# The token forms of the second down group: when their splits are issued in a hybrid encoder block

## The chip, the cores and the metric

The kernel runs on one core of a Trainium2 chip. The metric is the device time of one launch in microseconds (us). The engines of the core are TensorE (PE in the profile, with PEld for its weight loads), VectorE (DVE), ScalarE (ACT), GpSimd (POOL) and SyncE (SP). Each works through its own list of instructions in order and waits for the others by semaphores. DMAs are issued by SP, ACT and POOL.

## The reference

One layer over 512 tokens of width 2048, all in float32: an input projection, two attention mixers, an output projection, and a SwiGLU feed-forward part with a final norm. The change touches only the down projection, the last matrix product:

```python
h2 = rmsnorm(x, g_ffn[layer])
gate, up = jnp.split(jnp.einsum('bsd,df->bsf', h2, w_gate_up[layer]), 2, axis=-1)
x = x + jnp.einsum('bsf,fd->bsd', jax.nn.silu(gate) * up, w_down[layer])
return rmsnorm(x, g_final)
```

Here s is 512, d is 2048 and f is 5632.

## The kernel before

**Precision.** TensorE multiplies in a reduced type. So each float32 operand is split into a high half (a cast on ScalarE) and a low half (operand minus high half, on VectorE), and one product is three matmuls: high by high, high by low, low by high (lines 238 to 240).

**Fewer products.** The large products are computed by a scheme of Strassen's kind: a 2 x 2 block product with seven multiplications, named m1 to m7. Each needs one "form" of the tokens (a sum or difference of token blocks) and one of the weights. The token forms live in SBUF in the tiles `arena`, already split. The weight forms are made just before use: for m1, m2 and m3 a weight tile is taken as it was loaded; for m7, m6, m5 and m4 VectorE first makes a sum or difference of two tiles (line 837), and then the split follows (line 795 on ScalarE, line 798 on VectorE).

**Blocks and units.** A `ColBlock` covers a number of pairs of 128-row blocks of the inner dimension. A unit is one form with one pair: six matmuls of 128 x 512. The down projection's inner dimension is cut into three groups of 6, 8 and 8 pairs (`DOWN_PAIRS`), and each group has two blocks, one for each half of the output columns (cb 0 and 1). A block of 6 pairs has 42 units, one of 8 pairs 56. Within a block the units stand in the order m1, m7, m6, two units of m2, m5, the rest of m2, m4, m3. The weights of a unit are split about five units ahead of its matmuls (`COLS_AHEAD`), through a ring of eight tiles `tw`, so at unit n VectorE and ScalarE work on the weights of unit n + 5.

**PSUM.** Several forms share a bank: m1, m6, m5 and m3 one pair of banks, m7 and m4 a second, m2 a third. After the last unit of most forms, ScalarE copies the bank out (`ev`, line 1180) and GpSimd adds the copy to the result in DRAM by an accumulating DMA (`x1d`, line 1181). The next form on the same bank may start only when the copy is done.

**Token forms of the next group.** The gate/up part stores all token forms in DRAM. The arena holds one group's forms at a time, so while the second column block of a group runs, and the first block of the next, `next_forms` brings in the next group's forms one by one: a DMA into a buffer `fr` (two buffers, issued by ScalarE, line 1154), the high half on ScalarE (line 1157) and the low half on VectorE (line 1160). A form of 8 pairs takes two such steps of 4 pairs (h = 0 and 1). So the second group has 14 steps. They are hung on units: `box.after(form, late, f)` runs f behind the matmuls of the unit that is `late` units after the last unit of that form in the block `box`.

**Weight loads.** SP issues one DMA of 256 KB for each weight tile (`raw`, line 267), some 15 units ahead at most and as far as buffers are free. The loads of SP and the `fr` loads of ScalarE take their completion semaphores (DMAHW0 to DMAHW7) from one set of eight in turn. A DMA waits, on the engine that issues it, until the last DMA on its semaphore has landed.

Of the kernel before, what the change touches and what calls it, by code (L numbers as in the profile page):

```python
# [51 lines left out]
W_TILES = {"wi": 10, "wo": 12}  # L52
DOWN_PAIRS = (6, 8, 8)
ORDER = ("m1", "m7", "m6", "m2", "m4", "m5", "m3")
EARLY = 2
EVICT = 6
HEAD_RATE = (1.42, 1.9)
# [5 lines left out]
def f32(ap):  # L63
    return ap.bitcast(F32)
# [3 lines left out]
def encoder_block(ctx, tc, x, g_mix, w_in, g_q_a, g_k_a, g_out_a, g_out_b, w_out, g_ffn,  # L68
# [77 lines left out]
    gqk = turning[:, :2 * HD].rearrange("p (a c) -> p a c", a=2)  # L146
    arena = [sp.tile([P, n, 8, 2, 256], F32R, tag=f"arena{n}", bufs=1, name=f"arena{n}") for n in (EARLY, 7 - EARLY)]

    def form_tile(m, pairs):
        return arena[0][:, m, pairs] if m < EARLY else arena[1][:, m - EARLY, pairs]  # L150

    def form_pair(m, pairs, j):
        t, lo = (arena[0], m) if m < EARLY else (arena[1], m - EARLY)
        return t[:, lo:lo + 2, pairs, j]
# [93 lines left out]
    def in_turn(tiles, n, shape, dtype, tag):  # L248
        if not tiles and homing[0]:
            whole = sp.tile([P, n] + shape[1:], dtype, tag=tag + "s", bufs=1, name=nm(tag))  # L250
            tiles.extend(whole[:, i] for i in range(n))
        if not tiles:
            tiles.extend(sp.tile(shape, dtype, tag=tag, bufs=n, name=nm(tag)) for _ in range(n))
        tiles.append(tiles.pop(0))
        return tiles[-1]
# [49 lines left out]
    def hook(n, f):  # L305
        hooks.setdefault(n, []).append(f)
# [459 lines left out]
    def form_of(form, i):  # L766
        t = form_tile(ORDER.index(form), i)
        return t[:, 0], t[:, 1]
# [259 lines left out]
    def h_side(i, half, apart=False):  # L1028
# [12 lines left out]
        if half >= 2:  # L1041
            src = hpart[0][:, 256:].rearrange("p (f c) -> p f c", c=256)
            for t, part in ((arena[0], src[:, :EARLY]), (arena[1], src[:, EARLY:])):
                if half == 2:
# [91 lines left out]
    for f in range(0, NFF, 4):  # L1136
        box = gate_up_block(f)
# [6 lines left out]
    def next_forms(box, first, pairs):  # L1144
        seq = sorted(CHAIN, key=box.at.get)

        def ready(form, h):
            m, st = ORDER.index(form), {}
            lo_q, n = 4 * h, min(4, pairs - 4 * h)
            hi, lo = (form_tile(m, slice(lo_q, lo_q + n))[:, :, j] for j in range(2))  # L1150

            def load():
                st["t"] = in_turn(frs, 2, [P, 4, 256], F32, "fr")[:, :n]
                nc.scalar.dma_start(st["t"], forms_dram[:, m, first + lo_q:first + lo_q + n])

            def split_hi():
                nc.scalar.activation(hi, st["t"], AF.Copy)

            def split_lo():
                nc.vector.tensor_tensor(lo, st["t"], f32(hi), op=OP.subtract)  # L1160
            late = 4 * seq.index(form) + 4 * h
            box.after(form, late - 5, load)
            box.after(form, late + 1, split_hi)
            box.after(form, late + 3, split_lo)
        for form in seq:
            for h in range(-(-pairs // 4)):
                ready(form, h)
# [120 lines left out]
    first = 0  # L1288
    for n in DOWN_PAIRS:
        next_forms(box, first, n)  # L1290
        for cb in range(2):
            box = down_block(first, n, cb, (first + n, cb) == (NFF // 2, 1))
        first += n

    at = [0.0]
# [145 lines left out]
```

## Time and profile before

| what | us |
|---|---|
| median of 3 runs | 1996.07 (1995.02 to 1996.52) |
| the profiled execution | 1998.18 |
| its span, from the first to the last instruction | 1996.4 |
| TensorE busy in the span | 1979.4 |
| VectorE busy | 1560.5 |
| ScalarE busy | 1106.1 |

Busy time of TensorE is modelled, since matmuls are pipelined: a matmul of 512 columns is shown with 0.39 us, while the next one may start 0.23 us after it. So lost time is better read from the starts of matmuls than from the busy share. The mean granted clock of TensorE over the span is 0.998 of full speed. In the rows of the timeline the first number is the start in us from the begin of the span, the second the duration, and the bracket at the end tells how long the engine had been idle and what ended that.

### The profile page before, as it was taken

The page shows a single profiled execution, that of the slowest core. Times are in us where ns is not written, and L with a number is a line of the kernel's source. Part 1 is how long each engine was busy: PE and PEld are TensorE (multiplying, and loading weights), DVE is VectorE, ACT ScalarE, POOL GpSimd, SP SyncE. Part 2 cuts the span into 40 slices and gives each one's busy share as a digit, 9 for nine tenths or more (in the row PEclk, how much of TensorE's full clock was granted, in tenths as well). Part 3 has the DMA queues.
Part 4 walks back from the last instruction along what each step waited for, and adds up shares of the span by engine and source line. Part 5 has one row for each costly group of instructions (what it writes and reads, how often), then busy time and mean ns, then how long its engine had stood idle before and what let it go on. Part 6 is the DMA issues. An engine that isn't in the chain of part 4 may idle for free.

```text
span 1996.4 us, 27478 instructions
## 1 busy us (share of the span) xinstructions
PE 1979.4 (99%) x9020; PEld 1631.5 (82%) x9020; DVE 1560.5 (78%) x2787; ACT 1106.1 (55%) x1983; POOL 147.2 (7%) x191
## 2 busy tenths in 40 slices
PE   9999999999999999999999999999999999999998
PEld 7888888888888888888888888888888887788886
DVE  6887876668845698877878878878879987887968
ACT  7655345456543565554555555555556665666655
POOL 0000111101110000000000000000000121111121
PEclk9999999999999999999999999999999999999999
DMA  8576532335253555845836747647558799768864
GB/s 276 179 279 234 178 117 94 111 131 186 96 174 113 199 186 175 282 152 196 300 117 248 251 134 263 220 168 277 170 188 286 195 243 261 200 156 269 196 173 153
DMA packets 229216, 390.62 MB, mean 196 GB/s; under 512 B 21408, under 2 KB 70352, under 8 KB 228944
## 3 DMA queue, kind: packets, MB, share of 16 engines
q1 hardware_dynamic: 204592, 325.61, 48.2%
q0 software_dynamic: 17680, 41.95, 9.2%
q10 hardware_dynamic: 6800, 21.31, 3.1%
q8 instruction: 70, 1.15, 0.2%
q14 instruction: 74, 0.61, 0.1%
HBM read 325.08 MB, written 63.70 MB: 195 GB/s over the span
## 4 chain that ended last, share of the span: by engine, by line
PE 91%; DVE 4%; DMA 3%; issue 1%; ACT 1%; ACTq 0%; POOLq 0%; POOL 0%; DVEq 0%; SPq 0%
PE b L238 29%; PE b L240 29%; PE b L239 29%; DMA raw<-in_w_down_dram 3%; DVE tw L798 2%; PE b L595 1%; DVE raw L837 1%; PE b L1109 1%; DVE arena L1160 0%; PE b L1034 0%; PE b L548 0%; PE b L321 0%; ACT tw L795 0%; DVE x L1243 0%; DMA fixed<-in_c_ident_dram 0%
## 5 line engine op out<-in xcount | busy, mean ns | idle before, releaser
L238 PE MATMUL b<-tw,arena 128*128 128x512 f32 x2132 | 836.5, 392 | 2.5 <-ACT ev L1180 2.2
L239 PE MATMUL b<-tw,arena 128*128 128x512 f32 x2132 | 831.7, 390 | 2.8 <-DVE tw L798 2.2
L240 PE MATMUL b<-tw,arena 128*128 128x512 f32 x2132 | 831.1, 390 | 0.0
L795 ACT ACTIVATE tw<-raw 128x512 fp32r<-128x512 f32 x924 | 558.6, 628 | 438.8 <-DVE raw L837 286.5
L798 DVE TENSOR_TENSOR tw<-raw,tw 128x512 fp32r<-128x512 f32 x924 | 619.3, 687 | 174.4 <-ACT tw L795 171.8
L239 PEld LDWEIGHTS b<-tw,arena 128*128 128x128 f32 x2132 | 400.9, 188 | 88.3 <-DVE tw L798 6.1
L238 PEld LDWEIGHTS b<-tw,arena 128*128 128x128 f32 x2132 | 400.7, 188 | 84.9 <-ACT ev L1180 2.9
L240 PEld LDWEIGHTS b<-tw,arena 128*128 128x128 f32 x2132 | 400.6, 188 | 83.9
L837 DVE TENSOR_TENSOR raw<-raw,raw 128x512 f32<-128x512 f32 x528 | 361.8, 685 | 1.4 <-DMA raw<-in_w_gate_up_dram 1.2
L1181 POOL DMA_DIRECT2D x1d<-ev x76 | 66.5, 979 | 1151.8 <-ACT ev L1180 1139.5
L238 PE MATMUL b<-w,arena 128*128 128x512 f32 x368 | 146.3, 398 | 0.0
L240 PE MATMUL b<-w,arena 128*128 128x512 f32 x368 | 143.8, 391 | 0.0
L239 PE MATMUL b<-w,arena 128*128 128x512 f32 x368 | 143.4, 390 | 0.0
L229 ACT ACTIVATE pTh<-b 128x512 fp32r<-128x512 f32 x64 | 38.4, 599 | 118.2 <-PE b L595 115.6
L240 PEld LDWEIGHTS b<-w,arena 128*128 128x128 f32 x368 | 69.1, 188 | 15.1
L239 PEld LDWEIGHTS b<-w,arena 128*128 128x128 f32 x368 | 69.2, 188 | 13.9
L238 PEld LDWEIGHTS b<-w,arena 128*128 128x128 f32 x368 | 69.2, 188 | 13.7
L795 ACT ACTIVATE tw<-stage 128x512 fp32r<-128x512 f32 x92 | 56.0, 629 | 41.0 <-DVE stage L837 33.0
L295 DVE TENSOR_TENSOR w<-raw,w 128x512 fp32r<-128x512 f32 x96 | 66.1, 695 | 6.1 <-ACT w L290 4.0
L798 DVE TENSOR_TENSOR tw<-stage,tw 128x512 fp32r<-128x512 f32 x92 | 61.2, 686 | 8.6 <-ACT tw L795 8.5
L290 ACT ACTIVATE w<-raw 128x512 fp32r<-128x512 f32 x96 | 58.5, 626 | 14.4 <-PE b L240 6.9
L360 DVE TENSOR_TENSOR pair<-pair 128x256 f32<-128x256 f32 x120 | 45.5, 421 | 26.3 <-ACT pair L1037 25.3
(198 smaller groups left out, 1776.0 us busy)
## 6 DMA issues: line engine op xcount, KB each, us to landing
raw<-in_w_gate_up_dram SPq DMA_DIRECT2D x616, 256.0 KB, 5.3
raw<-in_w_down_dram SPq DMA_DIRECT2D x176, 256.0 KB, 6.5
stage<-in_w_in_dram SPq DMA_DIRECT2D x111, 256.0 KB, 5.3
forms<-pair SPq DMA_DIRECT2D x22, 896.0 KB, 5.3
x1d<-ev POOLq DMA_DIRECT2D x76, 256.0 KB, 6.6
fr<-forms ACTq DMA_DIRECT2D x35, 512.0 KB, 4.7
raw<-in_w_in_dram SPq DMA_DIRECT2D x64, 256.0 KB, 5.0
raw<-in_w_out_dram SPq DMA_DIRECT2D x32, 512.0 KB, 4.2
```

The lines of the kernel that those rows point to most:

```text
L229: nc.scalar.activation(hi, src, AF.Copy)
L238: nc.tensor.matmul(dst, ah, bh, start=start, stop=False, skip_group_check=chained)
L239: nc.tensor.matmul(dst, ah, bl, start=False, stop=False, skip_group_check=chained)
L240: nc.tensor.matmul(dst, al, bh, start=False, stop=stop, skip_group_check=chained)
L290: nc.scalar.activation(self.w[0], src, AF.Copy)
L295: nc.vector.tensor_tensor(self.w[1], self.src, f32(self.w[0]), op=OP.subtract)
L360: nc.vector.tensor_tensor(out, x, y, op=op)
L595: nc.tensor.transpose(ps[:, t * P:(t + 1) * P], self.p[t][:, kb * P:(kb + 1) * P], ident)
L795: nc.scalar.activation(self.pair[:, 0], self.src, AF.Copy)
L798: nc.vector.tensor_tensor(self.pair[:, 1], self.src, f32(self.pair[:, 0]), op=OP.subtract)
L837: nc.vector.tensor_tensor(t[dst], t[src[0]], t[src[1]], op=OP.add if form == "m6" else OP.subtract)
L1181: nc.gpsimd.dma_start(x1_dram[2 * cb + j, row], e, accum_op=OP.add)
```

## The change

Only the second group's steps move (`first` is 6, the first pair of that group). Before, the steps of a form start behind that form's last unit with a growing lag, four units for each step: the load at -5, the high half at +1, the low half at +3. After, a table `FORM_UNITS` gives for each form and each h the unit of the high half, counted from the first unit of the host block; the low half stands two units later, and the load four units earlier than the high half instead of six. The first group and the third keep the old rule.

```diff
+FORM_UNITS = {"m1": (11, 13), "m7": (19, 21), "m6": (29, 31), "m5": (35, 37), "m2": (41, 43), "m4": (58, 60), "m3": (68, 71)}
...
-            late = 4 * seq.index(form) + 4 * h
-            box.after(form, late - 5, load)
-            box.after(form, late + 1, split_hi)
-            box.after(form, late + 3, split_lo)
+            if first == DOWN_PAIRS[0]:
+                at = box.at["m1"] + 1 - box.pairs + FORM_UNITS[form][h]
+            else:
+                at = box.at[form] + 4 * seq.index(form) + 4 * h + 1
+            hook(at - (4 if first == DOWN_PAIRS[0] else 6), load)
+            hook(at, split_hi)
+            hook(at + 2, split_lo)
```

Counted in the same way, the units of the 14 high halves before were 6, 10 (m1), 16, 20 (m7), 26, 30 (m6), 38, 42 (m5), 46, 50 (m2), 56, 60 (m4), 66 and 70 (m3). The host block is units 0 to 41, and the second group's first block begins at unit 42. The weights that VectorE makes at units 13, 14, 21 to 24 and 31 to 44 need no sums, and neither do those at 61 and 62 and at 71 to 76. Apart from line numbers, the matmuls and the order of SP's and GpSimd's instructions stay as they were; what changes there is which of the eight semaphores a DMA takes.

## The prediction

> Units are counted from the first unit of the block that hosts the moved work (first group, second column half): units 0 to 41 are that block, 42 to 97 the second group's first block.
>
> **What bounds the kernel now.** I read the page first (its span), then the stretches of the down blocks, TensorE's waits there, and the rows around the longest ones.
>
> ```profile
> span 1996.4 us, 27478 instructions
> PE 1979.4 (99%) x9020; PEld 1631.5 (82%) x9020; DVE 1560.5 (78%) x2787; ACT 1106.1 (55%) x1983; POOL 147.2 (7%) x191
> ...
> 1616.30:1673.40 57.10, 57.10 (x253) 47.09 (x251) 43.94 (x66) 35.08 (x58) 12.19 (x14) 1.00 0.95 263
> 1673.40:1757.20 83.80, 80.04 (x338) 63.87 (x338) 67.08 (x101) 51.40 (x84) 12.25 (x14) 0.98 0.76 206
> 1757.20:1833.30 76.10, 76.10 (x337) 63.06 (x336) 63.42 (x96) 48.45 (x79) 12.27 (x14) 1.00 0.78 211
> ...
> PE b L239 <- DVE tw L798: 1.7, 4, 0.6
> PE b L238 <- ACT ev L1180: 1.7, 1, 1.7
> PE b L238 <- ACT tw L795: 0.3, 1, 0.3
> ```
>
> The window rows give length, then busy time of PE, PEld, DVE, ACT and POOL, granted clock, DMA share, GB/s. The host block is 42 units in 57.1 us, 1.36 us each; the third row is 56 units in 76.1, again 1.36. The second row, 56 units of the second group, takes 83.8: 7.7 us more. That is all the change can win here, and it lies behind unit 42. The waits name who is late: the weights' low halves (VectorE) and one eviction (ScalarE).
>
> ```profile
> 1673.17 0.39 PE L240 MATMUL b<-tw,arena 128*128 128x512 f32 x1
> 1673.87 0.49 PE L238 MATMUL b<-tw,arena 128*128 128x512 f32 x1 [0.31 <-ACT tw L795]
> 1674.60 0.50 PE L239 MATMUL b<-tw,arena 128*128 128x512 f32 x1 [0.23 <-DVE tw L798]
> ...
> 1711.57 0.50 PE L239 MATMUL b<-tw,arena 128*128 128x512 f32 x1
> ...
> 1714.67 0.70 PE L238 MATMUL b<-tw,arena 128*128 128x512 f32 x1 [1.66 <-ACT ev L1180]
> 1715.17 0.63 PE L239 MATMUL b<-tw,arena 128*128 128x512 f32 x1
> 1715.59 0.63 PE L240 MATMUL b<-tw,arena 128*128 128x512 f32 x1
> ...
> 1663.84 0.33 ACTq L1154 DMA_DIRECT2D fr<-forms  x1
> 1664.21 1.68 ACT L795 ACTIVATE tw<-raw 128x512 fp32r<-128x512 f32 x3 [2.82 <-PE b L239]
> 1665.79 1.25 ACT L1180 ACTIVATE ev<-b,smalls 128x512 f32<-128x512 f32 x2
> 1666.93 0.63 ACT L795 ACTIVATE tw<-raw 128x512 fp32r<-128x512 f32 x1
> 1672.81 0.33 ACTq L1154 DMA_DIRECT2D fr<-forms  x1
> 1673.18 1.15 ACT L795 ACTIVATE tw<-raw 128x512 fp32r<-128x512 f32 x2 [5.63 <-DMA raw<-in_w_down_dram]
> 1674.24 1.04 ACT L1157 ACTIVATE arena<-fr 128x1024 fp32r<-128x1024 f32 x1
> 1675.19 1.14 ACT L795 ACTIVATE tw<-raw 128x512 fp32r<-128x512 f32 x2
> ...
> 1662.20 10.52 DMA raw<-in_w_down_dram
> ```
>
> The first loss begins at unit 42 (1673.4). ScalarE sat 5.63 us ahead of it: its form load of 1672.81 waited until a weight load, issued at 1662.20, had landed 10.52 later, at 1672.72, and all splits behind it in ScalarE's order waited too. With the lead gone, VectorE must win it back in m7 and m6, whose weights need a sum:
>
> ```profile
> 1694.87 1.22 DVE L1160 TENSOR_TENSOR arena<-fr,arena 128x1024 fp32r<-128x1024 f32 x1
> 1696.01 0.68 DVE L837 TENSOR_TENSOR raw<-raw,raw 128x512 f32<-128x512 f32 x1
> 1696.61 0.68 DVE L798 TENSOR_TENSOR tw<-raw,tw 128x512 fp32r<-128x512 f32 x1
> 1697.21 0.68 DVE L837 TENSOR_TENSOR raw<-raw,raw 128x512 f32<-128x512 f32 x1
> ```
>
> From start to start a sum or a low half costs 0.60, a form's low half 1.14. A unit with a sum costs VectorE 1.20 of TensorE's 1.36 and wins back 0.16; one without wins 0.76. So a form half in the sums costs seven units' gain. At unit 68 TensorE also needs the bank that m6 leaves, and the eviction stands on ScalarE behind the splits of unit 70: from 1711.57 to 1714.67 are 3.10 us for five matmuls that take 5 x 0.23, a loss of some 1.85 with no lead.
>
> **The change, part by part.** The same 14 loads, 14 ScalarE halves and 14 VectorE halves run; nothing is added. VectorE behind unit 42, at the turn from m1 to m7 (raw<-raw,raw is a sum, arena<-fr a form's half), before:
>
> ```order
> L1160 TENSOR_TENSOR arena_86<-fr_12628,arena_86 128x4x256
> L837 TENSOR_TENSOR raw_14152<-raw_14150,raw_14152 128x512
> L798 TENSOR_TENSOR tw_6041<-raw_14136,tw_6041 128x512
> L837 TENSOR_TENSOR raw_14165<-raw_14163,raw_14165 128x512
> L798 TENSOR_TENSOR tw_6042<-raw_14152,tw_6042 128x512
> L837 TENSOR_TENSOR raw_14177<-raw_14175,raw_14177 128x512
> L798 TENSOR_TENSOR tw_6043<-raw_14165,tw_6043 128x512
> L837 TENSOR_TENSOR raw_14190<-raw_14188,raw_14190 128x512
> L798 TENSOR_TENSOR tw_6044<-raw_14177,tw_6044 128x512
> L1160 TENSOR_TENSOR arena_86<-fr_12627,arena_86 128x4x256
> ```
>
> and after:
>
> ```order
> L1161 TENSOR_TENSOR arena_86<-fr_12627,arena_86 128x4x256
> L799 TENSOR_TENSOR tw_6040<-raw_14127,tw_6040 128x512
> L838 TENSOR_TENSOR raw_14154<-raw_14152,raw_14154 128x512
> L799 TENSOR_TENSOR tw_6041<-raw_14137,tw_6041 128x512
> L1161 TENSOR_TENSOR arena_86<-fr_12628,arena_86 128x4x256
> L838 TENSOR_TENSOR raw_14166<-raw_14164,raw_14166 128x512
> L799 TENSOR_TENSOR tw_6042<-raw_14154,tw_6042 128x512
> ```
>
> From here through m6's sums before has four form halves, after two (this one and one behind the last sum): 2.3 us of VectorE less, the change's gain. Its price is on ScalarE. The sixth load (second half of m5), before:
>
> ```order
> L795 ACTIVATE tw_6041<-raw_13735 128x512 [waits Activation_49]
> L1154 DMA fr_12628<-forms 128x1024 [waits DMAHW7_49,DVE_49,Activation_49]
> L795 ACTIVATE tw_6042<-raw_14055 128x512 [waits DMAHW2_49]
> L795 ACTIVATE tw_6043<-raw_14067 128x512 [waits DMAHW3_49]
> L1157 ACTIVATE arena_86<-fr_12627 128x4x256 [waits DMAHW1_49]
> ```
>
> and after, with the weight loads on SP that matter:
>
> ```order
> L796 ACTIVATE tw_6038<-raw_13699 128x512 [waits PE_49]
> L1155 DMA fr_12628<-forms 128x1024 [waits DMAHW4_49,DVE_49,Activation_49]
> L796 ACTIVATE tw_6039<-raw_13711 128x512 [waits PE_49]
> ...
> L268 DMA raw_14205<-in_w_down_dram 128x512 [waits DMAHW4_49,DVE_49]
> L268 DMA raw_14207<-in_w_down_dram 128x512 [waits DMAHW5_49,DVE_49]
> L268 DMA raw_14217<-in_w_down_dram 128x512 [waits DMAHW6_49,DVE_49]
> L268 DMA raw_14219<-in_w_down_dram 128x512 [waits DMAHW7_49]
> ```
>
> The load moves from unit 36 to 33, ahead of the weights of unit 39 where it stood ahead of those of 42. The DMAs take eight semaphores in turn, and each waits for the last on its own; before it was DMAHW7, the load that landed at 1672.72, now DMAHW4, three weight loads earlier.
>
> ```profile
> 1638.77 32.76 SPq L267 DMA_DIRECT2D raw<-in_w_down_dram  x29
> ...
> q1 hardware_dynamic: 3522, 6.43, 57.2%
> q0 software_dynamic: 1082, 1.99, 31.9%
> q10 hardware_dynamic: 523, 1.88, 14.0%
> ...
> 1635.20 0.33 ACTq L1154 DMA_DIRECT2D fr<-forms  x1
> ...
> DMA to landing us min/median/max: 3.7/6.2/8.2
> ...
> DMA to landing us min/median/max: 3.7/4.1/4.5
> ```
>
> The 29 weight loads go out 1.13 us apart, and the three queues fill the engines (shares from 1638 to 1672). Three loads earlier is 1672.7 - 3.4 = 1669.3. The second half of m7's load (1635.20, ahead of the stream) now goes out behind unit 17's evictions, inside it; 14.0% of 34 us for three and a half form loads is 1.3 each. So 1669.3 to 1670.6; I take 1670.0.
>
> Step 1: before, 1.88 us pass from that landing to TensorE's second matmul (1674.60). Now 1671.9, where unit 39 is due at 1673.4 - 3 x 1.36 + 0.23 = 1669.55: **2.35 lost** (1.65 to 2.95 by the landing), where unit 42 lost 1.0. Behind the waiting load on ScalarE stand the weights of unit 39 on, m4's evictions (unit 35) and, through these, POOL's accumulating DMAs. Of them only the weights cost: m4's banks are opened again by m7 at unit 50, 15 units on, and nobody waits for the accumulation before the last blocks.
>
> On SP the moved loads count too, since weight loads follow them on the same semaphores: m7's second load now holds up one weight load (DMAHW0) for the time from about 1641 to its landing, some 6 us on, where before that place was free at 1645.8. With the engines full (57.2 + 31.9 + 14.0%) a later issue only reorders what they carry, so I put it at nothing; if the stream ran dry there it would add up to 1.5 to the 1670.0.
>
> Step 2: the form's high half now stands four units behind its load, not six. In the stream a form load lands after 6.2 (3.7 to 8.2; last two rows, from 1640 and up to 1640): 1670.1 + 6.2 + 0.95 (form half, 1674.24 to 1675.19) + 0.63 + 0.69 for unit 43's halves = 1678.6, due 1675.0: **3.6 late, 1.25 more** (with 3.7 nothing, with 8.2 it is 3.25).
>
> Step 3: to unit 50 VectorE runs three form halves (3.4), seven low halves (4.2) and two sums (1.2), and sits some 2.5 for ScalarE, which has a pair of evictions (1665.79 to 1666.93), a form half and a load that needs VectorE's own form half in it: 11.3, TensorE 9.5: **1.8 more**, between -0.7 (no sitting) and +4 (loads at 8.2).
>
> Step 4: 17 units to 67: 15 sums win 2.3, two units without 1.5, two form halves cost 2.3, evictions on ScalarE some 0.2: lead 1.3 of the 1.85 needed at unit 68: **0.5 lost**. The earlier splits (units 0 to 32) hide in the lead, as before; if it went, each costs at most its 1.14. The two loads of m4 and m3 find the DMAs calm.
>
> Sum 2.35 + 1.25 + 1.8 + 0.5, some 0.4 for slow first matmuls behind gaps: 6.3 against 7.7, **1.4 gained**. The span 1996.4 becomes 1995.0. The profiled execution took 1998.18, span and surroundings; the median 1996.07 lies under its span, so I take the difference off the median: **1994.7**.
>
> The half clock (0.43 from 1715.17 to 1715.59, against 0.23) came behind a gap of 2.05 us and is part of the 7.7. If unit 39's gap brings it too, TensorE runs slowly while it has to wait for splits anyway, so I add nothing; behind unit 68, where the lead is short, it would add up to eight matmuls x 0.2 = 1.6. The Trainium skill ("TensorE: Matmul & The Clock Gate", "What's actually happening") has the half rate only after an idle window of about 3.4 us. The trace disagrees: 2.05 were enough. By the page the sum stays as it is, and by the row 1.6 may come on top.
>
> **Rivals.** *Faster:* form loads land within 4.1, as outside the stream. Then step 2 ends at 1676.5, 1.5 late, inside the 2.35, and step 3 wins 0.7 back: 2.4 + 0.5 lost, **1991.2**. For it speaks 4.1 before 1640, against it 6.2 in the stream. The Trainium skill ("DMA: Bandwidth & Descriptors", "Anatomy of one DMA — SWDGE (gpsimd) path") fits 2.0 us plus bytes over 436 GB/s: an estimate of 3.2 for 512 KB, by which this rival would be the forecast; no load of these rows was under 3.7.
> *Slower:* they take 8.2. Unit 43 is 5.6 late, m2's first load goes out at 1679, lands at 1687, and unit 47 comes at 1689.3, due 1680.4: 8.9 late, 2.5 follow: 11.4, **1999.8**. It decides from 8 us on, the longest row of the stream.
> *No effect:* the order shows the halves moved; it would be 1996.1.
>
> **Chances.** Forecast and no effect, within 4 us (0.2%, about what measuring this kernel can tell): 0.58; faster rival 0.24; slower 0.18. The range takes both rivals' times in: 1990.8 to 2000.0; the forecast's own is 1992.5 to 1998.
>
> **What would show it.** Step 1: ScalarE idle before a form load that ends near 1670, first gap at unit 39, not 42. Step 2: ScalarE idle before form halves, up to 1678. Step 4: no gaps in m7 and m6, the one at unit 68 under 1 us. Wrong if 33's load finds its semaphore free, or the 56 units take under 79 us or over 86.

## The result, and the profile after

The changed kernel takes **2000.55 us** (median of 16 runs, 1998.82 to 2002.25), the kernel before 1996.80 beside it (16 runs, 1994.85 to 2000.98). The ratio is 1.0018, with a 95% interval of 1.0011 to 1.0025: slower by 3.75 us, where 1.4 us of gain were forecast. The time lies 0.55 us above the upper end of the range. The profiled execution took 2000.31 us.

First the page's span and busy times, then the windows of the down blocks (length, busy time of PE, PEld, DVE, ACT and POOL, granted clock, DMA share, GB/s), then TensorE's waits in them (in total, how many, the longest). The windows are those of the prediction, so that the rows can be compared:

```profile
span 1998.5 us, 27488 instructions
PE 1980.0 (99%) x9020; PEld 1631.3 (82%) x9020; DVE 1558.8 (78%) x2787; ACT 1107.2 (55%) x1983; POOL 147.1 (7%) x191
...
1616.30:1673.40 57.10, 54.55 (x233) 44.39 (x232) 42.31 (x64) 34.21 (x54) 10.45 (x12) 0.97 0.90 246
1673.40:1757.20 83.80, 81.69 (x352) 65.28 (x352) 67.92 (x104) 53.34 (x87) 13.98 (x16) 1.00 0.78 208
...
PE b L239 <- ACT tw L796: 2.8, 2, 2.3
PE b L240 <- DVE tw L799: 1.0, 3, 0.5
PE b L239 <- ACT ev L1184: 0.6, 1, 0.6
```

The line numbers have moved by one to four. The page's busy times hardly differ; the loss is idle time, and it has moved. Before, the host block (units 0 to 41) ran without a wait and all was lost behind it. Now the same window holds 233 matmul records instead of 253, its granted clock is 0.97, unit 42 starts only at 1678.59, 61.85 us behind unit 0, and the costliest wait is for a high half of weights from ScalarE. The eviction's wait has shrunk from 1.7 to 0.6.

Now the start of the weight stream on VectorE and SP, and ScalarE and TensorE around the first gap:

```profile
1636.06 1.22 DVE L1161 TENSOR_TENSOR arena<-fr,arena 128x1024 fp32r<-128x1024 f32 x1
...
1639.00 1.21 DVE L1161 TENSOR_TENSOR arena<-fr,arena 128x1024 fp32r<-128x1024 f32 x1
1640.13 0.68 DVE L838 TENSOR_TENSOR raw<-raw,raw 128x512 f32<-128x512 f32 x1
1640.73 0.68 DVE L799 TENSOR_TENSOR tw<-raw,tw 128x512 fp32r<-128x512 f32 x1
...
1641.44 33.29 SPq L268 DMA_DIRECT2D raw<-in_w_down_dram  x28
...
1661.82 1.06 ACT L1158 ACTIVATE arena<-fr 128x1024 fp32r<-128x1024 f32 x1 [1.97 <-DMA fr<-forms]
1662.78 1.14 ACT L796 ACTIVATE tw<-raw 128x512 fp32r<-128x512 f32 x2
1665.08 1.06 ACT L1158 ACTIVATE arena<-fr 128x1024 fp32r<-128x1024 f32 x1 [1.16 <-DMA fr<-forms]
1668.62 0.33 ACTq L1155 DMA_DIRECT2D fr<-forms  x1
1669.00 1.15 ACT L796 ACTIVATE tw<-raw 128x512 fp32r<-128x512 f32 x2 [2.85 <-DMA raw<-in_w_down_dram]
...
1666.96 0.40 PE L241 MATMUL b<-tw,arena 128*128 128x512 f32 x1
1669.68 0.49 PE L239 MATMUL b<-tw,arena 128*128 128x512 f32 x1 [2.32 <-ACT tw L796]
...
1671.42 0.63 PE L239 MATMUL b<-tw,arena 128*128 128x512 f32 x1
1671.85 0.63 PE L240 MATMUL b<-tw,arena 128*128 128x512 f32 x1
```

The chain reads from the top. Both low halves of m1 now run on VectorE just ahead of the low half that frees the second group's first weight buffer: it ends at 1641.41, and SP's first load goes out at 1641.44, 24.7 us behind unit 0 where it was 22.5 (1638.77; unit 0 starts at 1616.28 before and 1616.74 after). The 2.2 us are about two form halves of 1.14. Later ScalarE sits for the data of m7's second half (1.28) and of both m6 halves (1.97 and 1.16; the last two are shown), and then its load of m5's first half waits until 1668.62 for a weight load that was issued at 1657.76 and took 10.8 us (the row of DMA issues for that instant). The weights of unit 37 on stand behind it: TensorE's matmul of 1669.68 starts 2.72 us after the one before, and those behind it come at half clock (0.43 from start to start; the granted clock from 1671.0 to 1673.5 is 0.50).

```profile
raw<-in_w_down_dram SPq DMA_DIRECT2D x1, 256.0 KB, 10.8
```

At unit 68 TensorE sits idle for the bank for 0.61 us instead of 1.66, and there is no half clock:

```profile
1717.04 0.39 PE L241 MATMUL b<-tw,arena 128*128 128x512 f32 x1
1718.04 0.50 PE L239 MATMUL b<-tw,arena 128*128 128x512 f32 x1 [0.61 <-ACT ev L1184]
```

### The profile page after: what moved, and what is told of

It reads as the page before. It is cut to its first block, busy times and chain, and to the rows that moved or that the text cites. A ratio compares the mean times of both kernels' runs of the same rounds, so it can differ in the third digit from the quotient of the medians.

```text
span 1998.5 us, 27488 instructions
## 1 busy us (share of the span) xinstructions
PE 1980.0 (99%) x9020; PEld 1631.3 (82%) x9020; DVE 1558.8 (78%) x2787; ACT 1107.2 (55%) x1983; POOL 147.1 (7%) x191
## 4 chain that ended last, share of the span: by engine, by line
PE 94%; DVE 2%; DMA 2%; issue 1%; ACT 1%; ACTq 0%; POOLq 0%; DVEq 0%; POOL 0%; SPq 0%
PE b L239 30%; PE b L240 30%; PE b L241 30%; PE b L596 1%; PE b L1110 1%; DVE tw L799 1%; DMA raw<-in_w_down_dram 1%; DMA fr<-forms 1%; DVE raw L838 1%; PE b L1035 0%; PE b L549 0%; PE b L322 0%; DVE arena L1161 0%; DMA fixed<-in_c_ident_dram 0%; ACT tw L796 0%
## 5 line engine op out<-in xcount | busy, mean ns | idle before, releaser
L239 PEld LDWEIGHTS b<-w,arena 128*128 128x128 f32 x368 | 69.1, 188 | 13.6
```

The costliest lines, as they stand in the source:

```text
L239: nc.tensor.matmul(dst, ah, bh, start=start, stop=False, skip_group_check=chained)
```

## The experiments

The times are medians of 10 or 11 executions (5 for GpSimd's loads in the change, one for the second profile of before); the kernel before had medians of 1996.5 to 1997.6 beside them, and each ratio is to the one beside it. The edits are shown against the changed kernel. For the place of a loss I use one table. It is worked out from the starts of the first matmuls of units 0, 42, 56 and 70 in each trace: the time between them, less 57.12, 19.04 and 19.04 us, which is what the fastest traces show for 42 units and for 14. Units 70 to 97 take 38.1 to 38.2 us each time (38.9 in the kernel that loses 17.4, where the column "together" counts that too). A row is one execution, and the executions of one kernel spread over 2.4 to 6.5 us, so two rows that differ by less than 1 us are not told apart.

| kernel | units 0-41 lost | 42-55 | 56-69 | together | time, us | ratio and interval |
|---|---|---|---|---|---|---|
| before, first profile | 0.5 | 2.1 | 5.1 | 7.6 | | |
| before, second profile | 0.0 | 1.5 | 3.5 | 5.0 | 1996.67 | |
| the change | 4.7 | 3.3 | 0.9 | 9.0 | 2000.55 | 1.0018 (1.0011 to 1.0025) |
| early steps put back | 0.3 | 3.6 | 0.9 | 4.8 | 1997.50 | 1.0002 (0.9993 to 1.0011) |
| late steps put back | 4.1 | 1.1 | 3.5 | 8.7 | 2000.53 | 1.0016 (1.0007 to 1.0025) |
| m1 put back | 3.9 | 4.0 | 0.9 | 8.8 | 1999.98 | 1.0013 (1.0004 to 1.0022) |
| before, m1 moved | 1.6 | 2.1 | 3.5 | 7.2 | 1999.21 | 1.0014 (1.0005 to 1.0023) |
| early loads, m1 put back | 1.9 | 2.9 | 1.0 | 5.7 | 1997.38 | 1.0006 (0.9997 to 1.0014) |
| early loads | 4.8 | 2.6 | 0.9 | 8.4 | 1999.43 | 1.0014 (1.0005 to 1.0023) |
| GpSimd loads in the change | 13.6 | 2.1 | 1.0 | 17.4 | 2008.38 | 1.0060 (1.0048 to 1.0073) |
| GpSimd loads for m5 alone | 3.1 | 5.7 | 0.9 | 9.7 | 2000.73 | 1.0020 (1.0011 to 1.0029) |
| GpSimd loads in before | 0.0 | 0.0 | 4.0 | 4.0 | 1995.28 | 0.9992 (0.9983 to 1.0000) |
| wide places, ScalarE loads | 4.7 | 1.5 | 1.4 | 7.5 | 1998.08 | 1.0011 (1.0002 to 1.0020) |
| wide places, GpSimd loads | 0.0 | 0.0 | 0.4 | 0.4 | 1991.61 | 0.9976 (0.9967 to 0.9984) |

**How typical is the profile of before?** No edit; a second profile.

> The kernel before unchanged, for a second profile of it. The stretch of 98 units from the host block's first to the second group's first block's end took 140.9 us in the first profile; if that is typical, 139.9 to 141.9 here, and what lies ahead of it and behind it moves by 1 to 2 us from run to run. If the first profile was an outlier: under 139.5.

The stretch took 138.3 us, so of the two the first profile is the outlier; the second one's time, 1996.67, lies among the medians of before, the first one's, 1998.18, above them. The gap at unit 42 that the prediction began with isn't there: the load of m5's second half went out 55.5 us behind unit 0 instead of 56.5, ScalarE sat 4.14 us ahead of it instead of 5.63, and the lead covered that.

```profile
1672.82 0.33 ACTq L1154 DMA_DIRECT2D fr<-forms  x1
1673.20 1.15 ACT L795 ACTIVATE tw<-raw 128x512 fp32r<-128x512 f32 x2 [4.14 <-DMA raw<-in_w_down_dram]
...
PE b L238 <- ACT ev L1180: 1.7, 1, 1.7
PE b L239 <- DVE tw L798: 1.4, 3, 0.6
```

So some 5.0 us, not 7.7, were there to be won in an ordinary run, as far as two profiles tell. Against this profile the losses of the table agree with the measured times within 1.6 us for every kernel.

**Which half of the change costs?** Early steps (m1, m7, m6) put back:

```diff
-FORM_UNITS = {"m1": (11, 13), "m7": (19, 21), "m6": (29, 31), "m5": (35, 37), ...}
+FORM_UNITS = {"m1": (6, 10), "m7": (16, 20), "m6": (26, 30), "m5": (35, 37), ...}
-            hook(at - (4 if first == DOWN_PAIRS[0] else 6), load)
+            hook(at - (4 if first == DOWN_PAIRS[0] and form not in ("m1", "m7", "m6") else 6), load)
```

> The changed kernel with the steps of m1, m7 and m6 (six of 14) at the units and the load lead that they had before; m5, m2, m4 and m3 stay as changed. Theory A/B with the start of the weight stream (m1's halves at units 11 to 15 hold VectorE just when the second group's first load needs its buffer, so the stream starts 2.7 us later and every landing in it is 2.7 us later): the stream starts at 1638.8 again, the gap at unit 37 falls under 1 us, unit 42 starts near 1675, 1993 to 1996. If the lateness comes from m5's loads at units 31 and 33 themselves: the gap stays at 2 us or more, 1998 to 2000.

Late steps (m5, m2, m4, m3) put back:

```diff
+FORM_UNITS = {"m1": (11, 13), "m7": (19, 21), "m6": (29, 31), "m5": (38, 42), "m2": (46, 50), "m4": (56, 60), "m3": (66, 70)}
...
+            hook(at - (4 if first == DOWN_PAIRS[0] and form in ("m1", "m7", "m6") else 6), load)
```

> The changed kernel with the steps of m5, m2, m4 and m3 (eight of 14) at the units and the load lead that they had before; m1, m7 and m6 stay as changed. If the early steps cause the late stream: the stream starts at 1641.4 and the load of m5's second half at unit 36 waits for a landing near 1675 instead of 1672.7, the first loss behind unit 42 grows from 1.0 to 3 us, and VectorE has four form halves in the sums again, so that the eviction at unit 68 loses 2 us: 1998 to 2001. If m5's loads at units 31 and 33 are the cause: as before, 1995 to 1997.

The split is clean. The early steps alone lose what the whole change loses (1.0016), all of it in the host block, behind a gap of 1.99 us at unit 38 and not, as I had expected, behind unit 42. ScalarE's load of m5's first half stands ahead of it:

```profile
1670.75 0.33 ACTq L1155 DMA_DIRECT2D fr<-forms  x1
1671.12 1.67 ACT L796 ACTIVATE tw<-raw 128x512 fp32r<-128x512 f32 x3 [3.12 <-DMA raw<-in_w_down_dram]
...
1671.81 0.50 PE L239 MATMUL b<-tw,arena 128*128 128x512 f32 x1 [1.60 <-ACT tw L796]
```

The late ones alone are as fast as before (1.0002): they win 2.6 us at units 56 to 69, which was my reason for a gain, and give 2.1 back at 42 to 55, where m5's and m2's loads land late. The run with the early steps put back stayed above the 1996 that I expected at most; that second loss is more than the difference.

**The stream's start, or late loads?** The early steps do two things: m1's halves delay the stream by 2.2 us, and m7's second load and both of m6 go out inside the stream and only four units ahead of their halves. Four kernels take these apart. m1 alone put back:

```diff
-FORM_UNITS = {"m1": (11, 13), ...}
+FORM_UNITS = {"m1": (6, 10), ...}
+            hook(at - (4 if first == DOWN_PAIRS[0] and form != "m1" else 6), load)
```

> The changed kernel with m1's two steps alone at their old units and lead (load 6 units ahead of the high half, halves at units 6 and 10); the twelve other steps stay as changed. Theory S (stream start: VectorE's two m1 halves at units 13 and 15 stand ahead of the low half that frees the buffer of the second group's first weight load, so the weight stream starts 2.2 us later): the stream starts 22.5 us behind unit 0 as before, all its landings come 2.2 us earlier, the gap at unit 37 falls from 2.7 to under 1 us, and the time to 1997 to 1998. Theory L (form loads in the stream: m7's second half and both of m6 are issued at units 17, 25 and 27, inside the stream and only 4 units ahead of their halves): the waits of 1 to 2 us before m6's high halves stay, the gap stays at 1.5 us or more, 1999.5 to 2001.

The kernel before with m1 alone moved:

```diff
+FORM_UNITS = {"m1": (11, 13), "m7": (16, 20), "m6": (26, 30), "m5": (38, 42), "m2": (46, 50), "m4": (56, 60), "m3": (66, 70)}
+LOAD_LEAD = {("m1", 0): 4, ("m1", 1): 4, ("m7", 0): 3, ("m7", 1): 5}
...
+            hook(at - (LOAD_LEAD.get((form, h), 6) if first == DOWN_PAIRS[0] else 6), load)
```

> The kernel before with m1's two steps alone moved to units 11 and 13, as in the change (m7's two loads move to units 13 and 15, since they need m1's buffers; all other steps as before). Theory S: the stream starts 24.7 us behind unit 0, the load of m5's second half waits 2.2 us longer, the first gap comes at unit 40 or 41 with 2 us or more, and the time rises by 2 to 3 us, to 1999 to 2000. Theory L: as before within 1 us, 1997 to 1998.

Earlier loads for m7 and m6, with m1 put back:

```diff
+FORM_UNITS = {"m1": (6, 10), "m7": (19, 21), "m6": (29, 31), ...}
+LOAD_LEAD = {("m1", 0): 6, ("m1", 1): 6, ("m7", 0): 9, ("m7", 1): 7, ("m6", 0): 7, ("m6", 1): 7}
...
+            hook(at - (LOAD_LEAD.get((form, h), 4) if first == DOWN_PAIRS[0] else 6), load)
```

> All halves of m7, m6, m5, m2, m4 and m3 in the units of the change, m1 at its old units; only the loads of m7 and m6 go out earlier, 7 to 9 units ahead of the high half instead of 4 (units 10, 14, 22 and 24 instead of 15, 17, 25 and 27). Beside the run with m1 alone put back (host block 61.05 us, high half of m7 idle 4.51 and of m6 1.98 for its load). If the late data is the cause (the shortened load lead): these idle times go, the host block takes 57.1 to 58.2, and the time is 1996 to 1998. If the place of the halves themselves is the cause (VectorE and ScalarE lose the same time there): the host block stays at 60 to 61 and the time at 1999 to 2000.

Earlier loads with m1 left where the change put it:

```diff
+LOAD_LEAD = {("m7", 0): 6, ("m7", 1): 6, ("m6", 0): 7, ("m6", 1): 7}
...
+            hook(at - (LOAD_LEAD.get((form, h), 4) if first == DOWN_PAIRS[0] else 6), load)
```

> The changed kernel with only the loads of m7 and m6 issued earlier (units 13, 15, 22 and 24 instead of 15, 17, 25 and 27); m1's halves stay at units 11 and 13, so the weight stream still starts 24.7 us behind unit 0. The fourth of a two by two with the changed kernel (late start, late loads), the run with m1 put back (old start, late loads) and the one with earlier loads and m1 put back (old start, early loads; host block 59.02 us, 1997.4). If the late loads are the whole cause: host block 59 to 59.5, 1997 to 1998. If the late start adds what it added to the kernel before (2.2 us): host block 60.5 to 61.5, 1999 to 2000.

Either is enough, and they don't add up. Late start and late loads lose 4.7 us in the host block, late loads alone 3.9, the late start alone 4.8 (a host block of 61.9 us, over the 61.5 that I expected at most); without both it is 1.9 (I had expected at most 1.1, and what is left isn't explained), and the time can't be told from before. The medians say the same: against the kernel before beside them these are 3.75, 2.98, 2.91 and 0.77 us more. Moving m1 alone in the kernel before (m7's loads move along behind it) costs 2.2 us, as theory S had it, though the first gap came at unit 42 with 1.4 us and not at 40 or 41 with 2; there SP's stream starts 24.7 us behind unit 0, and the load of m5's second half goes out 57.7 us behind it instead of 55.5. Counted from unit 0, the weight loads of the stream land 1.8 to 3.0 us later than in the second profile of before, most of them some 2:

```profile
1642.22 28.04 SPq L269 DMA_DIRECT2D raw<-in_w_down_dram  x25
...
1675.20 0.33 ACTq L1156 DMA_DIRECT2D fr<-forms  x1
1675.57 1.15 ACT L797 ACTIVATE tw<-raw 128x512 fp32r<-128x512 f32 x2 [3.92 <-DMA raw<-in_w_down_dram]
```

Putting m1 back in the changed kernel brought the stream's start back too (22.5), but not the time: theory L was right there in the waits and the time, but the one gap of 2.7 us became two of 1.27 and 1.06, less than its 1.5.

Both routes meet at one place, ScalarE's load of m5's first half. It waits for the last weight load on its semaphore, which lands 47.9 us behind unit 0 in the second profile of before, at 49.3 without both, at 50.2 with late loads alone, at 51.7 with the late start alone and at 51.8 in the changed kernel; each time this load goes out 0.1 us after that. Here it is with late loads alone, with early loads and a late start, and with neither:

```profile
1648.83 1.06 ACT L1158 ACTIVATE arena<-fr 128x1024 fp32r<-128x1024 f32 x1 [4.51 <-DMA fr<-forms]
...
1664.26 1.06 ACT L1158 ACTIVATE arena<-fr 128x1024 fp32r<-128x1024 f32 x1 [1.98 <-DMA fr<-forms]
1666.16 0.33 ACTq L1155 DMA_DIRECT2D fr<-forms  x1
1666.53 1.15 ACT L796 ACTIVATE tw<-raw 128x512 fp32r<-128x512 f32 x2 [1.21 <-DMA raw<-in_w_down_dram]
```

```profile
1667.58 0.33 ACTq L1156 DMA_DIRECT2D fr<-forms  x1
1667.95 1.15 ACT L797 ACTIVATE tw<-raw 128x512 fp32r<-128x512 f32 x2 [4.68 <-DMA raw<-in_w_down_dram]
```

```profile
1666.41 0.33 ACTq L1156 DMA_DIRECT2D fr<-forms  x1
1666.79 1.15 ACT L797 ACTIVATE tw<-raw 128x512 fp32r<-128x512 f32 x2 [5.12 <-DMA raw<-in_w_down_dram]
```

Counted from each trace's unit 0 (1615.85, 1615.75 and 1617.03) this load goes out at 50.3, 51.8 and 49.4, in the changed kernel at 51.9, and the host block loses 3.9, 4.8, 1.9 and 4.7. With late loads ScalarE has already sat for m7's and m6's data (4.51 and 1.98 us); with the late start the whole stream runs later. The last two rows are nearly the same wait; what differs is when it ends against TensorE's place, 2.4 us earlier, and that is worth 2.9 us. Late loads alone delay the stream by another path, too: m7's second load lands 32.95 us behind unit 0, and SP, whose tenth weight load is next on the same semaphore, sits 4.6 us until then and sends it at 33.02, where it went at 29.6 in the second profile of before. Here are SP's waits for form loads from 1638 to 1650 (in total, how many, the longest):

```profile
SPq L268 <- DMA fr<-forms: 4.8, 2, 4.6
```

How much of the 3.9 us that path costs, beside ScalarE's waits for data, is not taken further apart.

**Is it ScalarE's queue?** The loads of the second group issued by GpSimd, in the changed kernel and in the kernel before (the same edit):

```diff
-                nc.scalar.dma_start(st["t"], forms_dram[:, m, first + lo_q:first + lo_q + n])
+                queue = nc.gpsimd if first == DOWN_PAIRS[0] else nc.scalar
+                queue.dma_start(st["t"], forms_dram[:, m, first + lo_q:first + lo_q + n])
```

> The second group's 14 form loads are issued by GpSimd instead of ScalarE, at the same units. Theory A (ScalarE's blocked loads: the loss is the form loads that wait on ScalarE for a weight load's landing, and hold the weights' high halves behind them): ScalarE's idle times before the high halves of units 37 to 42 shrink to what the form halves themselves wait for their data, the gap of 2.7 us at unit 37 falls under 1 us, and the time comes to 1992 to 1996. Theory B (late data: the form halves wait 1 to 3 us for loads that land late in the weight stream, whoever issues them): the gap stays at 1.5 us or more, 1998 to 2000. Theory C (VectorE's work alone sets the loss): no change, 2000.5.

> The kernel before with the same edit: the second group's form loads from GpSimd. Theory A: the 5.63 us of ScalarE ahead of unit 42 go, the first loss of 1.0 us goes with them and the lead is kept into m7, so that the eviction at unit 68 loses under 1 us instead of 1.85: 1990 to 1993. Theory B: the load of m5's second half then lands some 7 us after it is issued, in time for its half six units later: also under 1994. Theory C (the four form halves in m7's and m6's sums take VectorE's time whatever ScalarE did): the lead is used up all the same, the gap at unit 68 stays at 2 us, 1995 to 1996.

And for m5 alone:

```diff
+                queue = nc.gpsimd if first == DOWN_PAIRS[0] and form == "m5" else nc.scalar
```

> The changed kernel with the two loads of m5 alone issued by GpSimd, so that ScalarE no longer waits there for a weight load's landing (2.85 us idle ahead of unit 37) and the loads go out at units 31 and 33. If that wait on the shared semaphore is what costs: the gap of 2.7 us at unit 37 falls under 1 us, the host block from 61.85 to 59 or less, 1997 to 1998.5. If the lead is lost earlier, in the high halves of m6 that wait for their data: the gap stays over 2 us at unit 36 to 39, 1999.5 to 2001.

With the change's short lead the queue is no cure. In the first kernel the halves wait for their data up to 8.69 us, and 17.4 us are lost: late data as in theory B, but with 2008.38 us far beyond what any of the three theories had. For m5 alone the time can't be told from the change's: the gap at unit 37 went, and one of 2.32 us came at unit 41. The wait for the semaphore went, but GpSimd sent the loads only at 1666.05 and 1669.28, each 0.7 us after VectorE had ended m6's late halves and so freed the buffers, and the half then sat for its data:

```profile
1664.13 1.22 DVE L1162 TENSOR_TENSOR arena<-fr,arena 128x1024 fp32r<-128x1024 f32 x1
1667.40 1.22 DVE L1162 TENSOR_TENSOR arena<-fr,arena 128x1024 fp32r<-128x1024 f32 x1
...
1666.05 0.58 POOL L1156 DMA_DIRECT2D fr<-forms  x1 [0.77 <-DMA raw<-in_w_down_dram]
1669.28 0.55 POOL L1156 DMA_DIRECT2D fr<-forms  x1 [2.65 <-DMA raw<-in_w_down_dram]
...
1673.73 1.06 ACT L1159 ACTIVATE arena<-fr 128x1024 fp32r<-128x1024 f32 x1 [4.25 <-DMA fr<-forms]
```

The trace names a weight landing as what released GpSimd; the times speak for the buffers. So the semaphore isn't the only limit there: next come the buffers, and then the landing. With the longer lead of the kernel before the queue does help: nothing is lost up to unit 55, and the run is faster by 0.08%, at the edge of its interval. Units 56 to 69 still lose 4.0, all of it at units 67 to 69, and that is the whole of the loss. This is theory C: VectorE still has the four form halves in the sums. In the table the five rows with the late steps at the old places lose 3.5 to 5.1 there, and the nine with them moved 0.4 to 1.4:

```profile
PE b L238 <- ACT ev L1181: 1.7, 1, 1.7
```

**Both together.** Early steps as before, late ones in the units without sums but wider apart, so that two buffers allow loads five to seven units ahead; once with GpSimd's loads and once with ScalarE's:

```diff
+FORM_UNITS = {"m1": (6, 10), "m7": (16, 20), "m6": (26, 30), "m5": (35, 38), "m2": (42, 46), "m4": (58, 60), "m3": (68, 71)}
+LOAD_LEAD = {("m5", 0): 7, ("m2", 0): 5}
...
+            hook(at - (LOAD_LEAD.get((form, h), 6) if first == DOWN_PAIRS[0] else 6), load)
```

> Early steps as before (m1 at units 6 and 10, m7 at 16 and 20, m6 at 26 and 30), the late ones in units without sums but wider apart (m5 at 35 and 38, m2 at 42 and 46, m4 at 58 and 60, m3 at 68 and 71), each load 5 to 7 units ahead and issued by GpSimd. If the two losses are independent (ScalarE's blocked load at unit 42, and VectorE's form halves in m7's and m6's sums), both go: no gap until unit 68 and under 0.5 us there, no half clock: 1991 to 1993. If loads from GpSimd land too late for halves in units 35 to 46 (7 to 10 us in the stream): gaps of 1 to 3 us between units 37 and 48 return and it is 1994 to 1997.

> The fast version (early steps as before, late ones in units without sums and wider apart) with its loads issued by ScalarE instead of GpSimd. If the places of the halves and the longer load lead make its gain: within 1.5 us of it, 1991.5 to 1993. If the queue does: the load of m5's or m2's second half waits on ScalarE for a weight load's landing again, gaps of 1 us or more between units 37 and 48, 1994 to 1997.

With GpSimd's loads the kernel takes **1991.61 us**, 0.9976 of before (0.9967 to 0.9984): faster than both. Two halves still wait for their data (1.77 and 1.98 us), and the lead covers that. Up to unit 67 TensorE loses nothing, and at unit 68 a quarter of a microsecond:

```profile
span 1988.8 us, 27512 instructions
...
1670.13 1.06 ACT L1160 ACTIVATE arena<-fr 128x1024 fp32r<-128x1024 f32 x1 [1.77 <-DMA fr<-forms]
1676.51 1.06 ACT L1160 ACTIVATE arena<-fr 128x1024 fp32r<-128x1024 f32 x1 [1.98 <-DMA fr<-forms]
...
1708.25 0.39 PE L242 MATMUL b<-tw,arena 128*128 128x512 f32 x1
1708.74 0.50 PE L240 MATMUL b<-tw,arena 128*128 128x512 f32 x1
```

With ScalarE's loads at the same units it takes 6.5 us more, over the 1997 that I expected at most. The load of m5's second half is where it goes wrong, and the wait is the longest for a weight load in these 98 units of any trace; a gap of 3.12 us follows at unit 38:

```profile
1671.32 0.33 ACTq L1156 DMA_DIRECT2D fr<-forms  x1
1671.69 1.67 ACT L797 ACTIVATE tw<-raw 128x512 fp32r<-128x512 f32 x3 [8.81 <-DMA raw<-in_w_down_dram]
```

The load's buffer was free at 1664.23, when VectorE ended m6's second low half; it stands there 7.1 us longer, for the landing of a weight load on the shared semaphore. With GpSimd's loads the same halves at the same units wait under 2 us for their data and lose nothing. So here the wait on the shared semaphore is shown to cost by itself, with the reservation that the two kernels differ in the queue of all 14 loads.

## Why the prediction was wrong

The sum was 6.3 us lost against 7.7 before. The traces show 9.0 against 5.0. Point by point:

- **What fell: "the earlier splits (units 0 to 32) hide in the lead, as before".** This sentence of step 4, and with it "I put it at nothing" for what the moved steps do to SP's stream, is the failed step. I priced an early half at 1.14 us of VectorE and didn't follow what VectorE's halves hold up on SP: the buffer of the stream's first weight load. m1's two halves moved the start of the stream by 2.2 us; alone in the kernel before they made its landings some 2 us later and cost 2.2. And I counted the loads of m7 and m6 only as traffic for a later one, where their own halves waited 1.28, 1.97 and 1.16 us for them. The six early steps make up the whole slowdown (1.0016 against 1.0018): moved alone they lose 4.1 us in units 0 to 41, and with them put back these units lose 0.3.
- **Step 1, the first gap.** The kind of wait was right, a form load on ScalarE behind a weight load's semaphore; the load was m5's first half, not its second, and the gap came at unit 37, not 39. Its size was close: 2.72 us from start to start is 2.49 lost, 2.35 forecast. That it agreed is chance. With the early steps put back the path that I had priced is left alone; there the load of m5's second half goes out 51.2 us behind unit 0, not at the 53.7 that 1670.0 stands for, and no gap of this size follows. (I called that load the sixth; of the 14 it is the eighth.)
- **Slow matmuls behind the gap: mis-sized.** I gave 0.4 and argued that the half clock would hide behind TensorE's waits. Units 0 to 41 lost 4.7 in all, so some 2.1 lie behind the gap's 2.49. Behind the gap of 0.84 at unit 47, without half clock, the next two starts follow after 0.73 and 0.34, a loss of 0.6; here it was 0.73 and 0.59, and six at 0.43 followed, so that the half clock cost some 1.4 more. It didn't hide.
- **Steps 2 and 3.** 1.25 + 1.8 = 3.05 forecast, 3.3 measured at units 42 to 55. Right in kind, late halves behind late loads, but split otherwise: 0.8 at units 43 and 44, 2.4 from 47 to 50. The loads of m5 and m2 took 6.0, some 6.2 (its landing isn't told; its half started then), 7.0 and 4.8 us, where I took 6.2.
- **Step 4.** Right in kind: no gap from unit 51 to 67, no half clock at 68. It lost 0.9 where I had 0.5.
- **The base.** I took 7.7 us from one profile as what could be won. The second profile shows 5.0; the gap at unit 42 was that run's own. I noticed that the profiled execution lay 2 us over the median and took the difference off the total, where it belonged to the very stretch that I was pricing. So of the 5.4 us between forecast and traces (1.4 won against 4.0 lost), 2.7 are the sum and 2.7 are this. Even without the early steps nothing was won: the late ones alone lost 4.8 against 5.0.
- **The rivals.** The slower one gave 1999.8, close to the time, but by another way: loads of 8.2 us at units 42 to 50. They weren't that slow there, and most of the loss lies ahead of unit 42. That loads would land within 4.1 us was wrong.

## What to carry to other kernels

A step that moves past the start of a transfer stream has to be priced by what its engine releases, here a buffer, and not by its own length: two form halves on VectorE moved the start of the stream by 2.2 us, and its landings with it. A DMA issued by a compute engine's queue can hold that engine for someone else's transfer; where that engine feeds the bound, issue it far ahead and give it to a queue with nothing behind it. One alone didn't do here: the wide places with ScalarE's loads took 1998.08 us, GpSimd's loads with the change's short lead 2008.38, both together 1991.61. Take the loss that a change is to win from more than one profile, if it hangs on when single transfers land.

## What the runs showed of the hardware

**Half clock.** One length of a gap doesn't decide whether it comes. Over the traces of these kernels behind 1450 us, from start to start of two matmuls: seven gaps of 1.1 to 1.5 us brought no half clock; of seven gaps between 1.99 and 2.32, three did (1.99, 2.06, 2.09) and four did not (2.07, 2.07, 2.07, 2.32); all five of 2.7 and above did, with four to seven matmuls at 0.43. The kernel before shows both: 2056 ns with half clock in its first profile, 2070 ns without in its second, at the same unit. The Trainium skill ("TensorE: Matmul & The Clock Gate", "What's actually happening") says that the activity window runs freely and isn't tied to the program; a mixed outcome at one length fits that. Its length for the idle window, about 3.4 us, doesn't fit the half clock behind gaps of 1.99 to 3.12 us.

**Transfers in a full stream.** The landing times of the six form loads between 1640 and 1680, in the changed kernel (of one of the six it isn't told) and then in the fast version with GpSimd's loads:

```profile
DMA to landing us min/median/max: 6.0/7.0/8.9
```

```profile
DMA to landing us min/median/max: 6.4/6.6/10.3
```

In these two kernels none landed in under 6 us, by either queue, where I had left room for 3.7. GpSimd's loads weren't faster; the difference is that no split of weights stands behind them. The Trainium skill ("DMA: Bandwidth & Descriptors", "Anatomy of one DMA — SWDGE (gpsimd) path") fits 2.0 us plus bytes over 436 GB/s, by which 512 KB would be an estimate of 3.2; the traces show two to three times that in the stream.
